# A transformer block with 16 routed experts on one core: the choice of expert 0 in written order, the weight loads around its gather, and four units in plain fp32 where there were six

## The chip, the cores and the metric

One core of a Trainium2 chip. The core has TensorE (PE) for matmuls, VectorE (DVE), ScalarE (ACT), GpSimd (POOL) and a queue engine (SP) that issues transfers; 16 DMA engines move data between HBM and the on-chip memory. The metric is device time of one execution in microseconds (us), the median of several runs.

## The reference

One layer of a hybrid encoder block, for 1024 tokens of 1024 channels, in fp32. A first half (modulated norm, one input projection, a Fourier group and windowed attention, an output projection, a gated residual) gives x2. The second half is the part that matters here:

```
h2  = rmsnorm(x2) * (1 + sc2) + sh2
aff = softmax(h2 @ w_router)                 # 1024 tokens x 16 experts
g, idx = top_k(aff.T, 128)                   # each expert picks its 128 best tokens
xin = h2[idx]                                # gather, 16 x 128 x 1024
y   = (silu(xin @ w_gate) * (xin @ w_up)) @ w_down   # per expert, three 1024 x 1024 matrices
out = x2 + g2 * scatter_add(idx, y * g)
```

The expert weights are 16 x 3 matrices of 4 MB each, read once.

## The kernel before, in words

**Units.** Each 1024 x 1024 expert matrix is cut into four units of 256 rows (1 MB). The units are numbered in the order in which PE uses them: 0 to 3 gate of expert 0, 4 to 7 up of expert 0, 8 to 11 gate of expert 1, 12 to 15 down of expert 0, 16 to 19 up of expert 1, 20 to 23 gate of expert 2, and so on. `load` (L1090) brings the next unit into one of 13 raw buffers. `cut_unit` splits a unit into a high part (ACT, L86) and a low part (DVE, L87) of a reduced fp32 format; a product with split operands is three matmuls for each block (`mm3`, L81 to L83: high by high, high by low, low by high), 12 for a unit. The units in `PLAIN` (0 to 5 before) are not cut: PE multiplies them in plain fp32 (L1263), where the trace shows two matmul records for each block, 8 for a unit.

**Order of work.** `product` is called once for each unit n. It first takes some steps of a generator, `selection` (five steps for each unit with n < 9, three after that), then cuts units up to three ahead, then issues the matmuls. `selection` holds what is still to be done for the other experts while expert 0 runs: 4 empty steps, the split of expert 0's gathered tokens (DVE `t0l`), 3 empty steps, `gather(1)`, then the sort that finds all other experts' thresholds (8 rounds, 1 merge and 6 + 7 + 7 sorting steps, DVE), 7 empty steps, a small matmul (L1227), 7 empty steps, the counting of positions, `gather_a(2)`, 7 empty steps and `gather(2)`; after unit 20 the same for expert 3. That makes 57 steps before the step that issues `gather(2)`. From expert 4 on the gather is issued inside the loop over experts.

**A gather** compares positions with slot numbers (`oneh`, L1277; on DVE for experts 0 to 3, on POOL for the others), multiplies the result with `aux` (token numbers and the gate value in three bf16 parts) on PE (L1285), makes the token numbers (`idx`, DVE L1287), and issues an indirect transfer from POOL (L1289) that reads 128 rows of h2 into `xe` (one buffer). `flip` (L1304) transposes `xe` on PE and splits it; PE reaches the flip of expert e+1 after the third up unit of expert e, which for expert 2 is after unit 18. `put(e)` multiplies by the down matrix (units 12 to 15 for expert 0), scales on ACT (L1318), multiplies by g2 on POOL (L1319, two halves) and issues an indirect scatter-add from POOL (L1322).

**The choice of expert 0.** Attention's last token tile (tile 7) ends in `oproj`. Its two halves of 512 columns are added to x2 on DVE (L791, L792); x2 is transposed (`x2_flip`, L834) and multiplied by the router matrix (L850), then the softmax (L862 to L870) gives the last 128 rows of `aff`. A running sort of the first six tiles (`sorter`) has by then given a list of best values; `choose(0)` (L1168 to L1211) ranks the last two tiles against it and gives the positions of expert 0, then `gather(0)` follows. Tile 7's h2 is finished on DVE between the steps of the choice (`scaled`, L818) and stored by SP (L1242) behind the 11 unit loads that were issued by then (`EARLY` and `LATER`); the load of unit 11 (`HELD`) waits for gather 0's issue by way of a one-element POOL memset. `choose(1)`, expert 1's `oneh` and the cuts of units 6 and 7 follow on DVE.

**What fixes the order.** A scheduler orders each engine's instructions unless `in_order` pins them as written. Before: PE, DVE and POOL from gather 0 to the loop, and all engines inside the loop. The lines quoted are those that set the steps:

```
drain(itertools.islice(rest, 5 if n < 9 else 3))        # product
ahead(min(la, 1 + n // 2))
if u == 2 and e + 1 < NE: xn = flip(gs[e + 1][2], e + 1)  # loop, up units
if 0 < e < NE - 1: drain(put(e - 1, hT))                  # loop, before the up units
```

Of the kernel before, what the change touches and what calls it, by code (L numbers as in the profile page):

```python
# [19 lines left out]
D = 1024  # L20
# [25 lines left out]
def block_kernel(ctx: ExitStack, tc: tile.TileContext, t_in, out):  # L46
# [712 lines left out]
    lastx = []  # L759

    def oproj(t):
# [42 lines left out]
        x2s[t] = x2, rs  # L804

        def normed(c, prev):
            with tc.issue_after(prev.ins):
                DVE.scalar_tensor_tensor(h2[:, c], x2[:, c], rs, G2_r[:, c], op0=OP.mult, op1=OP.mult)
            DVE.tensor_tensor(h2[:, c], h2[:, c], sh2_r[:, c], op=OP.add)

        if t == NT - 1:
            with tc.issue_after(lastadd.ins):
                drain(srt)
            yield from tail(t, 1)

            def scaled(c, prev):
                with tc.issue_after(prev.ins):
                    DVE.scalar_tensor_tensor(h2[:, c], h2[:, c], rs, sh2_r[:, c], op0=OP.mult, op1=OP.add)  # L818

            scaled(slice(0, 512), after["aff"])  # L820
            after["kept"] = lambda kept: scaled(slice(512, D), kept)
        else:
            normed(slice(0, D), cur)
# [13 lines left out]
    def tail(t, b0=0):  # L837
        x2, rs = x2s.pop(t)
        p = None
        for b in range(b0, 2):  # L840
            if b0:
                p = pt()
                for kc in range(4):
                    PE.matmul(p[:, :16], x2Ts[t][:, kc, :], wrG[:, kc, :16], start=(kc == 0), stop=False)
# [3 lines left out]
        if b0:
            for kc in range(4, 8):
                PE.matmul(p[:, :16], x2T[:, kc, :], wrG[:, kc, :16], start=False, stop=(kc == 7))  # L850
        else:

            p = pt()
            for kc in range(8):
                g = 32 * (kc % 4)
                PE.matmul(p[g:g + 32, :128], wrG[:, kc, :], x2T[:, kc, :], start=(kc < 4), stop=(kc >= 4))
            gs_ = p3.tile([128, 128], F32, name="gsum", bufs=1)
            ACT.activation(gs_, p[:, :128], AF.Copy)
            p = pt()
            PE.matmul(p[:, :16], gs_, gsel[:, :16], start=True, stop=True)  # L860
# [6 lines left out]
        ACT.activation(ex, lg, AF.Exp, bias=mx, accum_out=sm)  # L867
# [4 lines left out]
        yield  # L872
# [72 lines left out]
    def sorter():  # L945
# [21 lines left out]
    def filler2():  # L967
        rate[0] = RATE2
        for t in range(NT):
            for i, _ in enumerate(oproj(t)):  # L970
# [4 lines left out]
                for _ in range(2 if t > 4 else 1):  # L975
                    next(srt, None)
# [97 lines left out]
    def load(m=None):  # L1074
# [41 lines left out]
    DVE.tensor_copy(tri, r1_f)  # L1116
# [5 lines left out]
    POOL.memset(ones_b, 1.0)  # L1122
# [42 lines left out]
    def choose(e):  # L1165
# [14 lines left out]
        after.pop("kept", lambda kept: None)(k0)  # L1180
# [53 lines left out]
    gate_parts(0, OLD, DVE)  # L1234
# [45 lines left out]
    def gather(e, oneh=None):  # L1280
        if oneh is None:
            oneh = gather_a(e)
        p = pt()
        for t in range(NT):
            PE.matmul(p[:, :6], oneh[:, t, :], aux[:, t, e, :], start=(t == 0), stop=(t == NT - 1))  # L1285
# [3 lines left out]
        after["p"] = POOL.indirect_dma_start(out=xe, out_offset=None, in_=h2d,  # L1289
                                in_offset=bass.IndirectOffsetOnAxis(ap=idx[:, :1], axis=0))  # L1290
        ax = wk.tile([128, 6], F32, name="ax", bufs=2)
        DVE.tensor_copy(ax, p[:, :6])
        gt = wk.tile([128, 2], F32, name="gt", bufs=4)
        DVE.tensor_tensor(gt[:, 0:1], ax[:, 3:4], ax[:, 4:5], op=OP.add)  # L1294
        after["v"] = DVE.tensor_tensor(gt[:, 1:2], gt[:, 0:1], ax[:, 2:3], op=OP.add)
        gs[e] = idx, gt[:, 1:2], xe
# [29 lines left out]
    tp = traced()  # L1326
    gather(0)
# [30 lines left out]
    in_order(tp, "PE", "DVE", "Pool")  # L1358
    in_order(tsp, "SP")
# [29 lines left out]
    in_order(t2, *PINNED)  # L1389
# [67 lines left out]
```

## Time and profile before

| | us |
|---|---|
| median of 3 runs (983.13 to 985.94) | 984.17 |
| the profiled execution, its own time | 986.08 |
| span of the profiled execution, first to last instruction | 984.3 |
| PE busy, all of the span | 934.3 |
| DVE busy | 788.5 |
| ACT busy | 628.5 |
| POOL busy | 403.9 |

Busy times overlap. A row of the timeline gives start, duration, engine, line, operation, tiles written and read, shapes, count, and in brackets the idle time of the engine before it with what ended it. PEclk is the granted TensorE clock as a share of full speed (2.4 GHz); 0.50 is the lower level (1.2 GHz). Matmuls are pipelined, so a matmul's duration is longer than the distance to the next one. Line numbers are those of the kernel before.

### The profile page before, as it was taken

Reading aid. Unit: us, or ns where it says so; the run is one execution under the profiler, and the core shown is the slowest. Engines: PE = TensorE matmul, PEld = TensorE weight load, DVE = VectorE, ACT = ScalarE, POOL = GpSimd, SP = SyncE. Lnnn points to the kernel's source line nnn. Section 1 sums busy time; section 2 is a strip of 40 time slices with the busy share of each in tenths; the row PEclk is TensorE's granted clock in tenths of the full one; section 3 lists DMA queues with packets and bytes.
Section 4 is the critical chain, followed back from the end, with each engine's and each line's share of the span. In section 5 each row is a group of like instructions: output and inputs, shape, how many; then the busy total and the mean of one; then the engine's idle time right before and its main releaser. Section 6 shows DMA issues by size and latency. Waiting matters only on the chain.

```text
span 984.3 us, 13194 instructions
## 1 busy us (share of the span) xinstructions
PE 934.3 (95%) x4751; PEld 737.0 (75%) x4751; DVE 788.5 (80%) x1238; ACT 628.5 (64%) x838; POOL 403.9 (41%) x240
## 2 busy tenths in 40 slices
PE   4999999989999998799899999999999999999996
PEld 2678776757777776468788888888888888888885
DVE  1436787788777968888888988998898898899894
ACT  2464533667565653147577777777777878777872
POOL 1007465100000001103339768766976976782201
PEclk9999999989999998699899999999999999999998
DMA  8978566462222258699999999999999999999912
GB/s 289 342 254 278 173 214 219 130 190 81 94 77 85 74 193 320 265 406 391 332 341 410 383 386 407 389 386 385 411 386 385 408 386 389 393 403 386 385 72 43
DMA packets 91641, 283.95 MB, mean 288 GB/s; under 512 B 8140, under 2 KB 25728, under 8 KB 91448
## 3 DMA queue, kind: packets, MB, share of 16 engines
q1 hardware_dynamic: 86712, 266.32, 71.1%
q0 software_dynamic: 4864, 16.80, 6.7%
q8 instruction: 37, 0.61, 0.2%
q14 instruction: 28, 0.23, 0.1%
HBM read 263.79 MB, written 21.40 MB: 290 GB/s over the span
## 4 chain that ended last, share of the span: by engine, by line
PE 56%; DMA 1%; DVE 1%; issue 0%; POOLq 0%; ACT 0%; DVEq 0%
PE pa L81 17%; PE pa L83 17%; PE pa L82 17%; PE pt L1304 3%; PE pa L1263 2%; DMA out_dram<-ys,idx 1%; DVE wl L87 0%; DMA xe<-h2d,idx 0%; PE pt L1285 0%; PE pt L1339 0%; POOLq L1453 0%; DVE oneh L1277 0%; DVE ys L1321 0%; PE pa L1149 0%; DVE t1l L87 0%
## 5 line engine op out<-in xcount | busy, mean ns | idle before, releaser
L87 DVE TENSOR_TENSOR wl<-raw,wh 128x2048 fp32r<-128x2048 f32 (+1 forms) x189 | 422.4, 2266 | 55.7 <-ACT wh L86 54.7
L86 ACT ACTIVATE wh<-raw 128x2048 fp32r<-128x2048 f32 (+1 forms) x189 | 355.3, 1896 | 74.8 <-PE pa L82 62.0
L1277 POOL TENSOR_SCALAR oneh<-tri_f,pos 128x128 bf16<-128x128 f32 x96 | 210.4, 2206 | 15.2 <-PE pt L1285 14.7
L81 PE MATMUL pa<-wh,t1h 128*128 128x512 f32 x384 | 151.4, 394 | 0.0
L83 PE MATMUL pa<-wl,t1h 128*128 128x512 f32 x384 | 149.6, 390 | 0.0
L82 PE MATMUL pa<-wh,t1l 128*128 128x512 f32 x384 | 149.5, 389 | 0.0
L81 PE MATMUL pa<-wh,t0h 128*128 128x512 f32 x360 | 143.5, 399 | 0.0
L83 PE MATMUL pa<-wl,t0h 128*128 128x512 f32 x360 | 141.2, 392 | 0.0
L82 PE MATMUL pa<-wh,t0l 128*128 128x512 f32 x360 | 141.2, 392 | 0.0
L83 PEld LDWEIGHTS pa<-wl,t1h 128*128 128x128 f32 x384 | 72.1, 188 | 15.2
L82 PEld LDWEIGHTS pa<-wh,t1l 128*128 128x128 f32 x384 | 72.1, 188 | 14.3
L81 PEld LDWEIGHTS pa<-wh,t1h 128*128 128x128 f32 x384 | 72.1, 188 | 14.3
L803 POOL TENSOR_TENSOR rs<-ss,mhalf 128x1 f32<-128x1 f32 x8 | 4.4, 556 | 185.3 <-DVE ss L801 161.2
L83 PEld LDWEIGHTS pa<-wl,t0h 128*128 128x128 f32 x360 | 68.1, 189 | 14.5
L81 PEld LDWEIGHTS pa<-wh,t0h 128*128 128x128 f32 x360 | 68.3, 190 | 13.7 <-issue 0.2
L82 PEld LDWEIGHTS pa<-wh,t0l 128*128 128x128 f32 x360 | 68.2, 190 | 13.7 <-issue 0.2
L1289 POOL DMA_INDIRECT xe<-h2d,idx x16 | 18.2, 1139 | 139.9 <-DVE gt L1294 133.3
L1319 POOL TENSOR_TENSOR ys<-ys,g_r 128x512 f32<-128x512 f32 x28 | 50.0, 1803 | 46.0 <-ACT ys L1318 46.0
L1322 POOL DMA_INDIRECT out_dram<-ys,idx x15 | 49.3, 3288 | 45.9 <-DVE ys L1321 41.8
L278 ACT ACTIVATE hf<-pt,sh1c,G1c 128x128 f32<-128x128 f32 (+1 forms) x56 | 22.6, 482 | 34.9 <-PE pt L271 34.9
L376 PE MATMUL pu<-wh,hh 128*128 128x512 f32 x128 | 42.6, 417 | 1.0 <-ACT hh L86 0.9
L689 DVE CUSTOM_DVE_ANT_0 sb<-lg,bias,sink 128x384 f32<-128x384 f32 (+1 forms) x64 | 35.3, 579 | 9.9 <-PE lg L687 4.8
(329 smaller groups left out, 1630.8 us busy)
## 6 DMA issues: line engine op xcount, KB each, us to landing
raw<-in_w_gate_dram SPq DMA_DIRECT2D x64, 1024.0 KB, 9.3
raw<-in_w_up_dram SPq DMA_DIRECT2D x64, 1024.0 KB, 8.9
raw<-in_w_down_dram SPq DMA_DIRECT2D x63, 1024.0 KB, 9.1
raw<-in_w_ada_dram SPq DMA_DIRECT2D x16, 1024.0 KB, 7.8
raw<-in_w_ada_dram SPq DMA_DIRECT2D x16, 512.0 KB, 9.6
xt<-in_x_dram SPq DMA_DIRECT2D x8, 512.0 KB
raw<-in_w_out_dram SPq DMA_DIRECT2D x4, 1024.0 KB, 4.9
raw<-in_x_dram SPq DMA_DIRECT2D x8, 512.0 KB
```

Of the source, the lines that this page charges most:

```text
L81: PE.matmul(o, lh, rh, start=start, stop=False)
L82: PE.matmul(o, ll, rh, start=False, stop=False)
L83: return PE.matmul(o, lh, rl, start=False, stop=stop)
L86: ACT.activation(hi, src, AF.Copy)
L87: return (eng or DVE).tensor_tensor(lo, src, hi.bitcast(F32), op=OP.subtract)
L278: ACT.activation(hf[:, a * w:a * w + w], tp[:, a * w:a * w + w], AF.Identity, scale=G1c[:, kc:kc + 1], bias=sh1c[:, kc:kc + 1])
L376: PE.matmul(acc[:, :c1 - c0], lhs, r[kc][:, c0:c1], start=first, stop=(kc == 7 and r is w_l), skip_group_check=c0 == 1024)
L689: DVE.tensor_tensor_reduce(sb[:, :wid], lg[:, :wid], bias[:, kv * 4 + i, j0:j0 + wid], 1.0, sk[:, i:i + 1], op0=OP.add, op1=OP.max, accum_ ...
L1277: (POOL if t < shared else DVE).tensor_scalar(oneh[:, t, :], slots, pos[:, t, e:e + 1], None, op0=OP.is_equal)
L1304: PE.transpose(p[:, k * 128:k * 128 + 128], src[:, (4 * b + k) * 128:(4 * b + k + 1) * 128], ident)
L1319: POOL.tensor_tensor(ys[:, cs_], ys[:, cs_], g2_r[:, cs_], op=OP.mult)
L1322: POOL.indirect_dma_start(out=out2, out_offset=bass.IndirectOffsetOnAxis(ap=idx[:, :1], axis=0), in_=ys, in_offset=None, compute_op=OP.add)
```

## The change

The last tile gets a function of its own (`last_tile`). Its second half goes through the residual, the transposes and ACT's copy in two pieces of 256 columns; its square sum moves from ACT to DVE; the scaling of its h2 moves from DVE to ACT and the addition of sh2 to POOL, with the store in two halves. Small preparations (`tri`, `rank1`, the token part of `aux`) move from DVE to POOL; all gate parts of `aux` move to POOL, behind gather 0, so that gather 0 multiplies by the two token columns alone and expert 0's gate values come from a second small product at the start of `selection`. Expert 1's `oneh` moves into `selection`, behind the split `t0l`. Nine units are loaded before gather 0's end instead of eleven: unit 7 and all behind it wait for the gather's data, by a one-element POOL copy out of `xe`. Units 0 to 3 are plain; 4 and 5 are the two that are cut ahead, 6 and 7 are cut in the loop. `product` takes five steps of `selection` for n < 4 and three after that; the running sort of the last tiles takes four steps at a time for tiles 6 and 7. PE, DVE and POOL are pinned as written from the last tile's first step to the end, SP from the store on, ACT in the loop.

```diff
-EARLY, LATER, HELD = (6, 7, 2, 3, 9, 10), (0, 1, 4, 5, 8), 11
-
-PLAIN = range(6)
-HOME3, HOME2 = (6, 7, 2, 3), (0, 1, 4, 5, 8)
+EARLY, LATER, HELD = (4, 5, 2, 3, 9, 10), (0, 1, 6), 7
+
+PLAIN = range(4)
+HOME3, HOME2 = (4, 5, 2, 3), (0, 1, 6, 7, 8)
...
-    def in_order(start, *engines):
+    def in_order(start, *engines, free=()):
...
-            if e in engines:
+            if e in engines and i.name not in free:
...
+    def last_tile(t, rows, x2, h2, o, ss):
+        mark.append(traced())
+        x2T = x2Ts.pop(t)
+        p = pj()
+        for kc in range(4):
+            PE.matmul(p[:, :16], x2T[:, kc, :], wrG[:, kc, :16], start=(kc == 0), stop=False)
+        for q in range(2):
+            c = slice(512 + 256 * q, 768 + 256 * q)
+            DVE.tensor_tensor(h2[:, c], o[:, 256 * q:256 * q + 256], g1_r[:, c], op=OP.mult)
+            DVE.tensor_tensor(x2[:, c], x2[:, c], h2[:, c], op=OP.add)
+            f = pt()
+            for k in range(2):
+                PE.transpose(f[:, k * 128:k * 128 + 128], x2[:, c.start + k * 128:c.start + k * 128 + 128], ident)
+            ACT.activation(x2T[:, 4 + 2 * q:6 + 2 * q].rearrange("p a b -> p (a b)"), f[:, :256], AF.Copy)
+        for kc in range(4, 8):
+            PE.matmul(p[:, :16], x2T[:, kc, :], wrG[:, kc, :16], start=False, stop=(kc == 7))
+        junk = at0.tile([128, 512], BF, name="junk", tag="qn1")
+        DVE.scalar_tensor_tensor(junk, x2[:, 512:], 1.0 / D, x2[:, 512:], op0=OP.mult, op1=OP.mult, accum_out=ss[:, 1:2])
+        after["ss"] = DVE.tensor_tensor(ss[:, 0:1], ss[:, 0:1], ss[:, 1:2], op=OP.add)
+        rs = p3.tile([128, 1], F32, name="rs", bufs=2)
+        POOL.tensor_tensor(rs, ss[:, 0:1], mhalf[:, 0:1], op=OP.pow)
+        DVE.tensor_tensor(h2[:, 512:], x2[:, 512:], G2_r[:, 512:], op=OP.mult)
+        R, = ranked
+
+        def aside():
+            ACT.activation(h2[:, :512], h2[:, :512], AF.Copy, scale=rs)
+            for b in range(3):
+                DVE.transpose(bestw[32 * b:32 * b + 32, :], R[:, 32 * b:32 * b + 32])
+
+        affinity(t, p, rs, aside)
+        DVE.transpose(bestw[96:, :], R[:, 96:])
+        POOL.tensor_copy(bestT, R[:16])
+        with tc.issue_after(after["exp"].ins):
+            ACT.activation(h2[:, 512:], h2[:, 512:], AF.Copy, scale=rs)
+        for c in (slice(0, 512), slice(512, D)):
+            POOL.tensor_tensor(h2[:, c], h2[:, c], sh2_r[:, c], op=OP.add)
+        lastx.append((rows, x2, h2))
...
-                for _ in range(2 if t > 4 else 1):
+                for _ in range(4 if t > 5 else 2 if t > 4 else 1):
...
-            with tc.issue_after(after["p"].ins):
-                POOL.memset(r[0:1, 0, 0:1], 0.0)
+            POOL.tensor_copy(r[0:1, 0, 0:1], gs[0][2][0:1, 0:1])
...
+    def gate_parts():
+        POOL.memset(aux[:, :, :, 5], 0.0)
+        POOL.tensor_copy(aux[:, :, :, 2], aff)
+        POOL.tensor_tensor(r1, aff, aux[:, :, :, 2], op=OP.subtract)
+        POOL.tensor_copy(aux[:, :, :, 3], r1)
+        POOL.tensor_tensor(r1, r1, aux[:, :, :, 3], op=OP.subtract)
+        POOL.tensor_copy(aux[:, :, :, 4], r1)
...
-    gate_parts(0, OLD, DVE)
     for m in LATER:
         load(m)
     (rows, x2, h2), = lastx
     tsp = traced()
-    gate_parts(OLD, NT, POOL)
-    c0 = choose(0)
-    next(c0)
-    SP.dma_start(h2d[rows, :], h2)
+    for hf in range(2):
+        SP.dma_start(h2d[rows, hf * 512:hf * 512 + 512], h2[:, hf * 512:hf * 512 + 512])
     SP.dma_start(out2[rows, :], x2)
-    drain(c0)
+    drain(choose(0))
...
-        drain(itertools.islice(rest, 5 if n < 9 else 3))
+        drain(itertools.islice(rest, 5 if n < 4 else 3))
...
     gs = {}
-    tp = traced()
-    gather(0)
+    oneh0 = gather_a(0)
+    gather(0, oneh0)
+    gate_parts()
     while len(raws) < NR:
         load()
     SP.dma_start(g2_r, md[3:4, :].to_broadcast([128, D]))
     drain(choose(1))
-    oneh = gather_a(1)
-    cut_unit(2)
-    cut_unit(2)
+    for n, c in (("ax", 4), ("gt", 2)):
+        wk.tile([128, c], F32, name=n, bufs=2 * (4 // c))
+    with tc.issue_after(after["exp"].ins):
+        cut_unit(2)
+        cut_unit(2)
...
     def selection():
+        p = pt()
+        for t in range(NT):
+            PE.matmul(p[:, :4], oneh0[:, t, :], aux[:, t, 0, 2:], start=(t == 0), stop=(t == NT - 1))
+        gates(0, p[:, :4])
         yield from wait(4)
         split(xh, xl, xf)
+        oneh = gather_a(1)
         yield from wait(3)
         gather(1, oneh)
...
     rest = selection()
-    in_order(tp, "PE", "DVE", "Pool")
-    in_order(tsp, "SP")
     t2 = traced()
...
-    in_order(t2, *PINNED)
+    in_order(mark[0], "PE", "DVE", "Pool", free=[i.ins.name for i in aside])
+    in_order(tsp, "SP")
+    in_order(t2, "Activation")
```

`affinity` is the softmax part of `tail`, unchanged, and calls `aside` before the exponential; `gates` is the gate part of `gather`, unchanged but for its columns; `ranked` holds the sort's result.

## Rows read from the trace of the kernel before

**Rows 1.** Windows answer: stretch, length, busy us per engine (instructions), PEclk, DMA share, GB/s.
```profile
478.20:482.10 3.90, 0.34 (x10) 0.31 (x8) 3.90 (x4) 2.50 (x3) 0.00 (x0) 0.77 1.04 418
482.10:487.40 5.30, 5.30 (x15) 4.18 (x14) 2.97 (x6) 0.32 (x1) 5.15 (x6) 0.52 0.96 363
487.40:960.00 472.60, 472.60 (x2274) 391.63 (x2273) 422.55 (x293) 367.61 (x272) 310.54 (x143) 1.00 0.97 371
```

**Rows 2.** Waits, 370 to 500 us: waiter <- releaser: us in total, times, longest.
```profile
PE pt L1285 <- DVE t1l L87: 3.6, 1, 3.6
...
PE pt L1339 <- DMA xe<-h2d,idx: 2.9, 1, 2.9
```

**Rows 3.** Timeline of DVE, 366 to 440 us: start, us, engine, line, operation.
```profile
384.81 0.67 DVE L791 TENSOR_TENSOR raw<-lg,g_r 128x512 f32<-128x512 f32 x1
...
390.52 0.23 DVE L862 SCALAR_TENSOR_TENSOR lg<-pt,rs,cb 128x16 f32<-128x16 f32 x1 [1.20 <-PE pt L850]
...
393.41 0.74 DVE L818 SCALAR_TENSOR_TENSOR raw<-raw,rs,sh_r 128x512 f32<-128x512 f32 x1
...
394.47 0.22 DVE L1187 SCALAR_TENSOR_TENSOR edge<-pa,rank,best 128x1 f32<-128x1 f32 x1
...
398.77 0.22 DVE L1287 TENSOR_SCALAR idx<-pt 128x1 int32<-128x1 f32 x1 [0.28 <-PE pt L1285]
...
405.20 4.62 DVE L87 TENSOR_TENSOR wl<-raw,wh 128x1024 fp32r<-128x1024 f32 x4
...
411.88 0.22 DVE L1287 TENSOR_SCALAR idx<-pt 128x1 int32<-128x1 f32 x1 [0.92 <-PE pt L1285]
```

**Rows 4.** Timeline of PE, 366 to 432 us.
```profile
383.88 0.40 PE L83 MATMUL lg<-wol,yah 128*128 128x512 f32 x1
...
388.53 1.89 PE L850 MATMUL pt<-wrG,x2T 128*128 128x16 f32 x8 [0.69 <-ACT x2T L835]
...
411.81 17.33 PE L1263 MATMUL pa<-raw,ys 128*128 128x512 f32 x40
```

**Rows 5.** Timeline of all engines, 392 to 414 us.
```profile
394.18 0.34 SPq L1242 DMA_DIRECT2D h2d<-raw  x1
...
401.02 1.12 POOL L1289 DMA_INDIRECT xe<-h2d,idx  x1 [6.39 <-DVE junk L1175]
```

**Rows 6.** Groups of DVE, 411.9 to 434.8 us: busy, mean ns | idle before.
```profile
L87 DVE TENSOR_TENSOR wl<-raw,wh 128x2048 fp32r<-128x2048 f32 x2 | 4.6, 2278 | 1.7 <-ACT wh L86 1.7
...
L87 DVE TENSOR_TENSOR t1l<-pt,t1h 128x512 fp32r<-128x512 f32 x2 | 1.3, 686 | 1.0 <-ACT t1h L86 1.0
```

**Rows 7.** Timeline of DVE, 430 to 500 us.
```profile
434.57 0.22 DVE L1224 TENSOR_SCALAR dg<-ident,R 16x16 f32<-16x16 f32 x1
```

**Rows 8.** Timeline of PE, 455 to 492 us.
```profile
459.95 0.39 PE L81 MATMUL pa<-wh,t1h 128*128 128x512 f32 x1
...
468.12 1.04 PE L1304 MATMUL pt<-ident,xe 128*128 128x128 f32 x8
```

**Rows 9.** Timeline of POOL, 450 to 490 us.
```profile
454.10 0.94 POOL L1289 DMA_INDIRECT xe<-h2d,idx  x1 [40.77 <-DVE gt L1294]
460.25 3.61 POOL L1319 TENSOR_TENSOR ys<-ys,g_r 128x512 f32<-128x512 f32 x2 [5.22 <-ACT ys L1318]
464.14 3.38 POOL L1322 DMA_INDIRECT out_dram<-ys,idx  x1 [0.28 <-POOL ys L1319]
482.25 6.82 POOL L1277 TENSOR_SCALAR oneh<-tri_f,pos 128x128 bf16<-128x128 f32 x8 [14.73 <-PE pt L1285]
```

**Rows 10.** Line L1289, 480 to 960 us: gathers of later experts, issue to landing.
```profile
DMA to landing us min/median/max: 7.4/8.0/9.0
```

**Rows 11.** Chain that ended last: start us, us, what.
```profile
401.02 4.34 DMA xe<-h2d,idx
...
967.40 6.64 DMA out_dram<-ys,idx
```

**Rows 12.** The page's part 5: a POOL group beside busy DVE; busy, mean ns.
```profile
L1277 POOL TENSOR_SCALAR oneh<-tri_f,pos 128x128 bf16<-128x128 f32 x96 | 210.4, 2206 | 15.2 <-PE pt L1285 14.7
```

More of the change, by code (lines that the diff above doesn't have):

```diff
@@ L804, in oproj @@
         x2s[t] = x2, rs
[L806 to L823, printed above, removed]
@@ L824, in oproj @@
-        if t < NT - 1:
-            SP.dma_start(h2d[rows, :], h2)
-        else:
-            lastx.append((rows, x2, h2))
+        with tc.issue_after(cur.ins):
+            DVE.scalar_tensor_tensor(h2, x2, rs, G2_r, op0=OP.mult, op1=OP.mult)
+        DVE.tensor_tensor(h2, h2, sh2_r, op=OP.add)
+        SP.dma_start(h2d[rows, :], h2)
+    def last_tile(t, rows, x2, h2, o, ss):
[14 more added lines that the diff above has]
+            PE.matmul(p[:, :16], x2T[:, kc, :], wrG[:, kc, :16], start=False, stop=(kc == 7))
+        junk = at0.tile([128, 512], BF, name="junk", tag="qn1")
+        DVE.scalar_tensor_tensor(junk, x2[:, 512:], 1.0 / D, x2[:, 512:], op0=OP.mult, op1=OP.mult, accum_out=ss[:, 1:2])
[16 more added lines that the diff above has]
+        lastx.append((rows, x2, h2))
@@ L835, in x2_flip, with tail @@
         ACT.activation(x2Ts[t][:, 4 * b:4 * b + 4].rearrange("p a b -> p (a b)"), p, AF.Copy)
-    def tail(t, b0=0):
+    def tail(t):
         x2, rs = x2s.pop(t)
[L839 to L844, printed above, removed]
+        for b in range(2):
             x2_flip(t, b, x2)
@@ L847, in tail, with affinity @@
         x2T = x2Ts.pop(t)
[L848 to L860, printed above, removed]
+        p = pt()
+        for kc in range(8):
+            g = 32 * (kc % 4)
+            PE.matmul(p[g:g + 32, :128], wrG[:, kc, :], x2T[:, kc, :], start=(kc < 4), stop=(kc >= 4))
+        gs_ = p3.tile([128, 128], F32, name="gsum", bufs=1)
+        ACT.activation(gs_, p[:, :128], AF.Copy)
+        p = pt()
+        PE.matmul(p[:, :16], gs_, gsel[:, :16], start=True, stop=True)
+        affinity(t, p, rs)
+        yield
+    def affinity(t, p, rs, aside=None):
         lg = p3.tile([128, 16], F32, name="lg", bufs=2)
@@ L952, in sorter @@
         R = yield from halve(R)
-        for b in range(4):
-            DVE.transpose(bestw[32 * b:32 * b + 32, :], R[:, 32 * b:32 * b + 32])
-        DVE.tensor_copy(bestT, R[:16])
+        ranked.append(R)
     def wo_cut():
@@ L1115, in block_kernel @@
     SP.dma_start(r1_f, t_in["k_tri"][0])
-    DVE.tensor_copy(tri, r1_f)
+    aside = [POOL.tensor_copy(tri, r1_f)]
     tri_f = rt.tile([128, 3, 128], F32, name="tri_f")
@@ L1121, in block_kernel @@
     ones_b = rt.tile([128, 128], BF, name="ones_b")
[L1122 removed]
+    aside.append(POOL.memset(ones_b, 1.0))
     tok = rt.tile([128, NT, 2], F32, name="tok")
@@ L1278, in gather_a, with gather @@
         return oneh
-    def gather(e, oneh=None):
-        if oneh is None:
-            oneh = gather_a(e)
+    def gather(e, oneh):
+        n = 6 if e else 2
         p = pt()
         for t in range(NT):
-            PE.matmul(p[:, :6], oneh[:, t, :], aux[:, t, e, :], start=(t == 0), stop=(t == NT - 1))
+            PE.matmul(p[:, :n], oneh[:, t, :], aux[:, t, e, :n], start=(t == 0), stop=(t == NT - 1))
         idx = wk.tile([128, 1], I32, name="idx", bufs=4)
@@ L1288, in gather, with gates @@
         xe = wk.tile([128, D], F32, name="xe", bufs=1)
[L1289 removed]
+        POOL.indirect_dma_start(out=xe, out_offset=None, in_=h2d,
                                 in_offset=bass.IndirectOffsetOnAxis(ap=idx[:, :1], axis=0))
[L1291 to L1292 removed]
+        gs[e] = idx, None, xe
+        if e:
+            gates(e, p[:, 2:6])
+    def gates(e, p):
+        ax = wk.tile([128, 4], F32, name="ax", bufs=2)
+        DVE.tensor_copy(ax, p)
         gt = wk.tile([128, 2], F32, name="gt", bufs=4)
[L1294 to L1296 removed]
+        DVE.tensor_tensor(gt[:, 0:1], ax[:, 1:2], ax[:, 2:3], op=OP.add)
+        DVE.tensor_tensor(gt[:, 1:2], gt[:, 0:1], ax[:, 0:1], op=OP.add)
+        gs[e] = gs[e][0], gt[:, 1:2], gs[e][2]
     def flip(src, e):
```

36 lines of the change are left out of this document (17 added, 19 removed).

## The prediction

> **What bounds the kernel now.** I read the windows answer first. From 487.4 to 960 us PE is busy in all of its 472.6 us at full clock: a thread of matmuls that nothing else interrupts [rows 1]. So what is won or lost before expert 3 moves the end by as much, and only places where PE stands still, or runs at half clock, are to be looked at. The waits have two such places. PE waits for expert 0's gathered rows (end of the choice, 2.9 us of wait behind a long stretch of small work), and for 3.6 us at the product of gather 3, on a DVE flip half [rows 2]. The windows show that second one as 0.34 us busy in 3.9, and after it 5.3 us at a granted clock of 0.52, that is, mostly the 1.2 GHz level [rows 1]: another 2.6 us, so that gather 3 costs 6.2 in all.
>
> The timeline of the choice shows a chain through all engines: last matmul of tile 7 (383.88 + 0.40), DVE's additions to x2 (from 384.81), the router product at half clock (388.53, 1.89 us), the softmax (390.52), the last ranking steps (edge at 394.47), idx at 398.77, gather issued at 401.02, rows there 4.34 us later [rows 3, 4, 5, 11]. idx is finished at 398.99; the gather left 2.0 us after it, having waited for h2's store, which SP issued at 394.18 behind the last of eleven unit loads [rows 3, 5].
>
> **The change part by part.** All times are on the axis of the profiled execution (986.08 us; span 984.3 and 1.8 around it). It lies 1.9 above the median of 984.17; I add differences to the median.
>
> *Tile 7's tail and the choice.* DVE starts 0.5 us after PE's last matmul because sorting steps stand there, and its two operations on the last half have the sort's transposes between them. In pieces: start at about 384.4, four operations of 256 columns at half of 0.67 plus a dependent start, some 0.4 each, end 386.0. Two transposes instead of four, half a copy: the router product, of the same eight matmuls in 0.9 to 1.9 us, ends near 388.1, softmax at 388.2 in place of 390.5: 2.3 earlier. The 0.74 us that L818 takes in the choice goes to ACT; the edge gains 0.3 more, since the added best-list transposes run while ACT does the exponential. idx moves by -2.6 us. Bounds: -0.5 (four sorting steps at a time crowd DVE in tiles 6 and 7) and -3.3 [rows 3, 4].
>
> *Store and gather 0.* Two unit loads fewer stand ahead of the store, at 2.6 us each (1 MB at the 400 GB/s or so of the busy windows [rows 1]), so it ends by the new idx (396.4). Gather 0 leaves at about 396.7 and its rows are there at 401.0, 4.3 earlier. This is not what reaches PE's weights, next.
>
> *DVE up to gather 1.* From idx 0 to idx 1 DVE takes 13.1 us (398.77 to 411.88) [rows 3]: choice of expert 1, its `oneh`, 4.62 of cuts, the split. The same list stands in the new order; only `oneh` comes after the split, so PE's product for gather 1, written behind unit 0, now waits for all of it. Idx 1 is at 409.3, again -2.6; unit 0 ends at about 408. So 1.7 of the 4.3 is lost as a wait on PE. The moved gate parts (six POOL operations behind gather 0) and the extra eight small matmuls lie in the 5 us until the rows land, at 0.85 us an operation as in the `oneh` group that ran mostly beside an idle DVE (6.82 for 8 [rows 9]).
>
> *Loads.* Units 7, 8, 11, 12 leave near 403.5 and have 15 us or more before they are cut. Nothing; 2.6 us each if that cover were gone.
>
> *Two units cut instead of plain.* Plain: 17.33 for 40 records, 8 for a unit, 3.47 [rows 4]. Cut: three units from 459.95 to 468.12, 2.72 each [rows 8]. PE saves 2 x 0.75 = 1.5. DVE and ACT get two cuts more, at 2.28 on DVE [rows 6], and the cuts of 6 and 7 come where the sort is. DVE's list from idx 1 to `dg` (the operation behind the sort) was 22.9 us (411.88 to 434.79 [rows 3, 7]); without two cuts (4.6), their ACT wait (1.7), a flip half and its wait (1.3 and 1.0), 14.3 is the sort and its like [rows 6]. With the slower pace `dg` stands in unit 9, behind the cuts of 6 to 11: 14.3 + 6 x 2.28 + 1.3 (flip) + 1.3 (expert 0's product) = 30.6 us, and the cut of 12 and the flip half that frees PE's transposing buffer bring 33.5. PE is at unit 11 after 3 x 3.47 + 7 x 2.72 + 2 flips of 0.9 = 31.2. So DVE is late by about 2.3, where before it had room. I take 2.4; bounds 0 and 5. Units 11 to 15 and two small products of the counting are 5 x 2.72 + 1.2 = 14.8; unit 15 ends at idx 1 + 31.2 + 2.4 + 14.8 = 48.4 (before: 459.95 - 411.88 = 48.1 [rows 3, 8]), so at 457.8, 2.2 earlier than before: the 1.5 saved is eaten by the backlog.
>
> *The pace of `selection`.* This is the large term. 57 steps stand ahead of gather 2. Before, n = 0 to 8 take 45, n = 9 to 12 twelve: gather 2 falls into unit 13, and POOL issues it at 454.10 [rows 9], before `put(0)` is written. After, n = 0 to 3 take 20, n = 4 to 15 36: 56, so gather 2 falls into unit 16. On POOL's pinned queue it now stands behind `put(0)`: two multiplies (460.25, 3.61 us) and the scatter (464.14, 3.38 us) [rows 9], which begin only when unit 15 ends (459.95). POOL is free 7.6 us after unit 15, the gather leaves at 7.75, and lands 8.0 later (median of the thirteen later gathers, 7.4 to 9.0 [rows 10]): unit 15 + 15.75. PE comes to expert 2's flip after units 16 to 18, 8.5 after unit 15. It stands for 7.2 us. The flip starts at 457.8 + 15.75 = 473.5, before 468.12 [rows 8]: **+5.4**. Bounds of the landing: 4.34 as for gather 0 on an idle machine [rows 11], and 11.1 if the scatter's transfers, 6.64 from issue on a quiet end [rows 11], go first.
>
> *What the stop costs behind it.* After 3.6 us of standing, PE had 5.3 us at half clock [rows 1]; after 7.2 I take the same on 4.4 us: +2.2 (1.6 to 2.7).
>
> *Gather 3's stall.* PE comes to it later against DVE's list (flip half, cut, product, `oneh`, two cuts, flip half), which is unchanged: -1.5; bounds 0 and -6.2.
>
> Sum: +5.4 + 2.2 - 1.5 = **+6.1 us**: 990.3.
>
> A rule that speaks against the moved work: POOL's `oneh` operations take 2.21 us on average [rows 12], against 0.85 in the stretch of mostly idle DVE [rows 9]. The Trainium skill, "SBUF — State Buffer", section "SBUF: two separate sides", says that DVE operations with two SBUF inputs and GpSimd ones share a port pair under an exclusive lock, and the later one waits for the whole instruction. These rows agree in direction. The cuts are such operations, and by the rule the six gate parts would each wait for one (rival C).
>
> **The rivals.**
> - **A, one stall replaces the other: faster.** DVE works its backlog off in gaps and the drained queues let gather 2 land in 4.34. Unit 15 then ends at 409.3 + 31.2 + 14.8 = 455.3, the flip starts 12.1 later, at 467.4 (-0.7); +2.2 of clock; gather 3's stall and its half clock, 6.2, are gone: -4.7, 979.5. For it: front gains of 2.6 and 1.5 are real, and a long stop on PE lets DVE catch up. Against: later gathers never landed under 7.4 [rows 10]. It decides if PE starts expert 2's flip before 470.6.
> - **B, stall as forecast, gather 3 free: no change.** +5.4 + 2.2 - 6.2 = +1.4, 985.6. Against: DVE's list between the two is the same length.
> - **C, POOL blocked.** Six gate parts at 2.21 from 397.8 end at 411; the gate product on PE stands ahead of unit 0, which then ends 6 later than DVE allows; 2.4 of it pays DVE's backlog: +9.7, 993.9.
> - **D, the gather queues behind the scatter.** Its packets start when the scatter's are through (464.14 + 6.64 = 470.8, not 467.7): +3.1, in all +9.2, 993.4. The Trainium skill, "DMA: Bandwidth & Descriptors", section "Queues, rings and completion order", says that descriptors of one ring are taken in order, which is D; no row here has a gather directly behind a scatter.
> - That the change does not do what it says: the counts of steps follow from the code, and before's (gather 2 in unit 13) agrees with POOL's 454.10, one and a half units ahead of unit 16's 459.95 with idx behind the cuts [rows 8, 9]; I leave it nothing.
>
> **How the numbers follow.** Forecast 0.45, A 0.22, B 0.13, C 0.08, D 0.12. A change within 0.3% (2.95 us) can't be told from none. Slower: forecast, C and D, 0.65; same: B, 0.13; faster: A, 0.22. The forecast's own range is 987 to 994 (backlog 0 to 5, landing 4.34 to 11.1, one at its end at a time). The range for 8 in 10 cuts A's lower half and the sum of two bad ends: 979.5 to 996.5.
>
> **What would show it.** Right: PE idle for 5 us or more directly ahead of expert 2's flip (L1304's `xe`), released by a gather that POOL issues behind the scatter; a half-clock stretch after it; idx 0 some 2.6 earlier against tile 7's last matmul; PE waiting for DVE at gather 1 and around unit 11. Wrong: expert 2's flip without a wait, or gather 2 ahead of the scatter on POOL; then A or better holds.

## The result and the profile after

The changed kernel takes 997.25 us (median of six runs, 995.02 to 997.93) against 984.95 for the kernel before (six runs, 983.13 to 986.54): ratio 1.0115, 95% interval 1.0103 to 1.0127, that is 12.3 us slower. The forecast was +6.1. The profiled execution took 995.02, its span is 993.2. One execution of before_g3, a kernel further down, took 2383.70 us for a reason that nothing here shows; it counts in the median given there (988.29 without it) and not in the ratio.

The waits of PE between 360 and 500 us (waiter <- releaser: us in total, times, longest), for [rows 2]:

```profile
PE pt L1323 <- DMA xe<-h2d,idx: 10.1, 1, 10.1
PE pt L1245 <- DVE t0l L87: 2.9, 1, 2.9
...
PE pt L1299 <- DVE t1l L87: 1.7, 1, 1.7
PE pt L1299 <- DVE oneh L1292: 1.4, 1, 1.4
PE pt L1361 <- DMA xe<-h2d,idx: 1.3, 1, 1.3
```

L1323 is the flip (before L1304), L1299 the product of a gather (L1285), L1245 the small product behind the sort (L1227), L1361 expert 0's transposes (L1339). The 1.4 for `oneh` is at gather 0 (392.07 in PE's timeline below), where the kernel before waited 1.07; no wait of that list is at gather 1. The wait at gather 3 shrank from 3.6 to 1.7 and the one for expert 0's rows from 2.9 to 1.3; a new one of 2.9 stands behind the sort and a new one of 10.1 at expert 2's flip.

POOL's timeline, 383 to 500 us, for [rows 5, 9]:

```profile
385.71 2.50 POOL L852 TENSOR_TENSOR raw<-raw,sh_r 128x512 f32<-128x512 f32 x2 [0.59 <-ACT raw L842]
394.18 1.14 POOL L1303 DMA_INDIRECT xe<-h2d,idx  x1 [5.97 <-DVE idx L1301]
...
395.54 0.75 POOL L1153 CAST aux<-aff 128x128 bf16<-128x128 f32 x1
396.38 0.49 POOL L1154 TENSOR_TENSOR r<-aff,aux 128x128 f32<-128x128 f32 x1
...
458.35 3.81 POOL L1338 TENSOR_TENSOR ys<-ys,g_r 128x512 f32<-128x512 f32 x2 [49.36 <-ACT ys L1337]
462.44 3.45 POOL L1341 DMA_INDIRECT out_dram<-ys,idx  x1 [0.28 <-POOL ys L1338]
466.20 1.25 POOL L1303 DMA_INDIRECT xe<-h2d,idx  x1 [0.30 <-issue]
```

Gather 2 (466.20) stands behind `put(0)`'s multiplies and scatter; before it left ahead of them. The chain that ended last (start us, us, what) gives its landing, 10.56 us later, and what it released:

```profile
466.20 10.56 DMA xe<-h2d,idx
476.80 1.97 PE pt L1323 x8
```

PE's timeline: tile 7's last matmul, the product of gather 0, expert 0's transposes, the product of gather 1, the product behind the sort, and the first record behind unit 15, for [rows 4, 8]:

```profile
380.17 0.40 PE L83 MATMUL lg<-wol,yah 128*128 128x512 f32 x1
...
392.07 1.56 PE L1299 MATMUL pt<-aux,oneh 128*128 128x2 bf16 x8 [1.44 <-DVE oneh L1292]
...
398.69 1.61 PE L1361 MATMUL pt<-ident,xe 128*128 128x128 f32 x5 [1.27 <-DMA xe<-h2d,idx]
...
405.95 0.99 PE L1299 MATMUL pt<-aux,oneh 128*128 128x6 bf16 x8
...
441.33 0.51 PE L1245 MATMUL pt<-dg,ones 16*128 16x16 f32 x2 [2.94 <-DVE t0l L87]
...
458.06 0.35 PE L1299 MATMUL pt<-aux,oneh 128*128 128x6 bf16 x8
```

DVE's timeline, for [rows 3, 7]: start of the last tile's additions, the softmax's first and last operation, expert 0's edge, idx 0, the first cuts, idx 1, and the end of the sort:

```profile
381.23 0.41 DVE L825 TENSOR_TENSOR raw<-lg,g_r 128x256 f32<-128x256 f32 x1
...
385.09 0.23 DVE L883 SCALAR_TENSOR_TENSOR lg<-pj,rs,cb 128x16 f32<-128x16 f32 x1 [0.64 <-PE pj L832]
...
386.29 0.72 DVE L893 TENSOR_SCALAR aff<-ex,rsm 128x16 f32<-128x16 f32 x1
...
388.99 0.22 DVE L1205 SCALAR_TENSOR_TENSOR edge<-pa,rank,best 128x1 f32<-128x1 f32 x1
...
393.66 0.22 DVE L1301 TENSOR_SCALAR idx<-pt 128x1 int32<-128x1 f32 x1 [0.28 <-PE pt L1299]
...
406.99 0.22 DVE L1301 TENSOR_SCALAR idx<-pt 128x1 int32<-128x1 f32 x1 [0.28 <-PE pt L1299]
...
438.26 0.22 DVE L1242 TENSOR_SCALAR dg<-ident,R 16x16 f32<-16x16 f32 x1
438.41 2.27 DVE L87 TENSOR_TENSOR wl<-raw,wh 128x2048 fp32r<-128x2048 f32 x1
440.61 1.27 DVE L87 TENSOR_TENSOR t0l<-pt,t0h 128x512 fp32r<-128x512 f32 x2
```

Windows of the main stall, what follows it, the two shorter stretches at the lower clock, and the rest, for [rows 1] (same columns):

```profile
466.70:476.80 10.10, 0.00 (x0) 0.00 (x0) 2.08 (x1) 0.00 (x0) 0.75 (x1) 0.60 1.03 338
476.80:482.40 5.60, 5.60 (x17) 4.74 (x18) 2.54 (x3) 3.00 (x3) 0.00 (x0) 0.50 0.24 97
...
487.40:960.00 472.60, 470.87 (x2265) 389.93 (x2265) 421.82 (x295) 364.70 (x271) 315.52 (x148) 1.00 0.99 376
...
441.40:444.90 3.50, 3.50 (x9) 2.82 (x10) 3.50 (x5) 0.00 (x0) 0.00 (x0) 0.51 1.03 411
...
492.60:496.10 3.50, 3.50 (x10) 2.72 (x9) 2.15 (x1) 0.40 (x1) 3.50 (x3) 0.51 0.93 328
```

PE does nothing for 10.1 us, then works 5.6 us at half clock. From 487.4 on it is busy throughout, as before, but for the wait of 1.7 us at gather 3 and 3.5 us at half clock behind it; so what is lost ahead of the flip stays lost.

**Where the axes differ.** The two profiled spans differ by 8.9 us, the medians by 12.3. Tile 7's last matmul ends at 380.57, before at 384.28 [rows 4], 3.7 us earlier, though little of the change stands ahead of it. Some 3.4 of it are the clock of that one execution (19.00 us at 0.82, an estimate from the rows below): before's PEclk falls in a stretch of the attention where after's does not. The windows, of before and then of after:

```profile
199.00:218.00 19.00, 15.08 (x64) 10.11 (x65) 14.84 (x51) 11.14 (x31) 0.31 (x1) 0.82 0.73 221
```

```profile
199.00:215.00 16.00, 12.54 (x68) 8.22 (x69) 14.13 (x48) 10.63 (x31) 0.00 (x0) 1.00 0.73 229
```

The profiled execution of after is the fastest of its six runs, that of before near its slowest. From tile 7's end on, after loses 8.9 + 3.7 = 12.6 us, which agrees with the medians; below I count from there, in "marks": tile 7's end, idx 0, idx 1, end of unit 15 (458.06; before 459.95), flip of expert 2 (476.80; before 468.12), end.

### The profile page after: what moved, and what is told of

The parts are those of the page before. It is cut to its first block, busy times and chain, and to the rows that moved or that the text cites. A ratio compares the mean times of both kernels' runs of the same rounds, so it can differ in the third digit from the quotient of the medians.

```text
span 993.2 us, 13252 instructions
## 1 busy us (share of the span) xinstructions
PE 934.2 (94%) x4767; PEld 738.1 (74%) x4767; DVE 793.7 (80%) x1233; ACT 633.3 (64%) x841; POOL 408.7 (41%) x246
## 4 chain that ended last, share of the span: by engine, by line
PE 49%; DMA 2%; DVE 1%; issue 0%; POOLq 0%; DVEq 0%
PE pa L81 16%; PE pa L83 15%; PE pa L82 15%; PE pt L1323 3%; DMA xe<-h2d,idx 1%; DMA out_dram<-ys,idx 1%; DVE wl L87 0%; PE pt L1299 0%; POOLq L1480 0%; DVE ys L1340 0%; DVE oneh L1292 0%; DVE t1l L87 0%; DVEq L87 0%; DVEq L1340 0%; POOLq L1341 0%
## 5 line engine op out<-in xcount | busy, mean ns | idle before, releaser
L87 DVE TENSOR_TENSOR wl<-raw,wh 128x2048 fp32r<-128x2048 f32 (+1 forms) x191 | 427.1, 2266 | 54.4 <-ACT wh L86 53.4
L86 ACT ACTIVATE wh<-raw 128x2048 fp32r<-128x2048 f32 (+1 forms) x191 | 359.1, 1895 | 79.6 <-PE pa L82 63.9
L81 PE MATMUL pa<-wh,t0h 128*128 128x512 f32 x368 | 146.3, 397 | 0.0
L83 PE MATMUL pa<-wl,t0h 128*128 128x512 f32 x368 | 144.1, 392 | 0.0
L82 PE MATMUL pa<-wh,t0l 128*128 128x512 f32 x368 | 143.9, 391 | 0.0
```

The source lines that it names most:

```text
L81: PE.matmul(o, lh, rh, start=start, stop=False)
L82: PE.matmul(o, ll, rh, start=False, stop=False)
L83: return PE.matmul(o, lh, rl, start=False, stop=stop)
L86: ACT.activation(hi, src, AF.Copy)
L87: return (eng or DVE).tensor_tensor(lo, src, hi.bitcast(F32), op=OP.subtract)
```

## Experiments

Theory P: the loss is gather 2's place on POOL behind `put(0)`, and the pace of `selection` puts it there. Theory B: the loss is DVE's backlog, from the two added cuts. Every comparison is with the kernel before, run on the same chip.

**pace5: the change with one more unit at five steps.**

```diff
-        drain(itertools.islice(rest, 5 if n < 4 else 3))
+        drain(itertools.islice(rest, 5 if n < 5 else 3))
```

> The changed kernel with five steps of selection for n < 5 in place of n < 4: one unit's pace, two steps. Gather 2 falls into unit 15, so on POOL it stands ahead of put(0)'s multiplies and scatter. Theory P (the loss is gather 2's place behind put(0)): the 10.1 us wait at expert 2's flip goes but for 0 to 2 us, gather 2 leaves POOL before unit 16 starts, and the time falls from 997.3 to 986 to 989. Theory B (the loss is DVE's backlog from the two added cuts, and the flip only waits because everything is late): one unit earlier gives at most a third of the way, 993 or more.

Measured: 985.49 against 985.48, ratio 0.9999 (0.9989 to 1.0010). POOL's timeline:

```profile
457.13 0.94 POOL L1303 DMA_INDIRECT xe<-h2d,idx  x1 [46.18 <-DMA raw<-in_w_up_dram]
458.25 3.69 POOL L1338 TENSOR_TENSOR ys<-ys,g_r 128x512 f32<-128x512 f32 x2 [0.18 <-ACT ys L1337]
462.22 3.38 POOL L1341 DMA_INDIRECT out_dram<-ys,idx  x1 [0.28 <-POOL ys L1338]
```

Two more steps of a generator, which bring the gather out one unit earlier, 0.2 us before POOL takes up `put(0)`, are worth all of the 12 us. That is a net figure: the wait behind the sort is also shorter (1.8 us for 2.9, with no fall of the clock behind it), and gather 3's is back at 3.6. P's wait is gone as said; how much of the 12 is the backlog's, this run alone does not tell.

**pace9: the change with the pace of before (`n < 9`).**

> The changed kernel with five steps for n < 9, as in the kernel before. Gather 2 falls into unit 13. Theory P: no wait at expert 2's flip; the sort stands in more of the cuts, so PE waits up to 4 us for DVE around unit 8; 984 to 988. Theory B: with the two added cuts the faster pace makes DVE's backlog larger, and the time stays above 990.

Measured: 987.05, ratio 1.0018 (1.0007 to 1.0029). Gather 2 leaves earlier still (453.67), but PE now waits 3.1 us for `dg` at L1245 and has 3.4 us at half clock behind it: more steps early crowd DVE. It is the backlog that B speaks of, and the time is some 1.5 us over pace5's.

**before_pace4: the kernel before with the change's pace alone.**

```diff
-        drain(itertools.islice(rest, 5 if n < 9 else 3))
+        drain(itertools.islice(rest, 5 if n < 4 else 3))
```

> The kernel before with nothing changed but the pace: five steps for n < 4 in place of n < 9. Theory P: gather 2 falls into unit 16 behind put(0), expert 2's flip waits 8 to 11 us, 994 to 998, so the pace alone is the whole loss. Theory B: six plain units leave DVE room, the time stays within 3 us of 985.

Measured: 998.05, ratio 1.0135 (1.0115 to 1.0155). The first waits of PE, then POOL's timeline:

```profile
PE pt L1304 <- DMA xe<-h2d,idx: 9.7, 1, 9.7
```

```profile
460.95 3.80 POOL L1319 TENSOR_TENSOR ys<-ys,g_r 128x512 f32<-128x512 f32 x2 [47.94 <-DMA raw<-in_w_up_dram]
465.03 3.44 POOL L1322 DMA_INDIRECT out_dram<-ys,idx  x1 [0.28 <-POOL ys L1319]
468.77 1.26 POOL L1289 DMA_INDIRECT xe<-h2d,idx  x1 [0.30 <-issue]
```

The stall comes without any other part of the change: the pace alone gives it, and a loss of the same size.

**defer_scatter: the change, with `put(0)`'s scatter issued behind gather 2.** The two multiplies stay ahead of the gather.

> The changed kernel with put(0)'s scatter issued behind gather 2 in place of ahead of it; the two multiplies stay ahead. Gather 2 leaves POOL some 3.7 us earlier (the scatter's 3.45). Theory P with rival D (the gather's transfers also queue behind the scatter's): landing falls from 10.5 to about 8 us, the flip wait from 10.1 to about 4, the time by 6 to 991. P without D (the transfers are slow for another reason): landing stays at 10.5, the time falls by 3.7 to 993.5. Theory B: no change.

Measured: 989.63, ratio 1.0049 (1.0032 to 1.0067). The gather leaves at 464.66; its landing in the chain:

```profile
464.66 8.18 DMA xe<-h2d,idx
```

PE waits 3.8 us in place of 10.1. Pace, cuts and choice are those of the change, and 7.6 of the 12.3 us are gone. Of the 6.3 us that PE waits less, 3.9 come from the earlier issue (3.9 us behind POOL's first multiply in place of 7.85) and 2.4 from the landing (8.18 in place of 10.56).

The records of single DMA packets in the traces show what the scatter in front does. In the change, the scatter's packets of 4 KB (0.33 us each) start from 468.97 to 473.21, and the first of the gather's (0.16 us each) starts at 472.27, 6.1 us behind the gather's issue, when most of the scatter's are through. Gather 2 of the kernel before and of pace5, with no scatter in front, has its first packet 4.2 us behind the issue and lands 8.5 and 7.4 us behind it. So some 1.9 us of the landing are a wait behind the scatter's packets. In defer_scatter the first packet comes no sooner (6.3 us, of which POOL spends 2.93 on the issue), but all are through in 1.5 us in place of 3.9; why, no run here shows. The Trainium skill, "DMA: Bandwidth & Descriptors", section "Queues, rings and completion order", says for the queues of SP and ACT that each DMA engine takes descriptors in ring order; the packets here, from POOL's queue, agree.

**choice_alone: the change's last tile and choice, with the plain units, homes, loads and pace of before.**

```diff
-EARLY, LATER, HELD = (4, 5, 2, 3, 9, 10), (0, 1, 6), 7
-PLAIN = range(4)
-HOME3, HOME2 = (4, 5, 2, 3), (0, 1, 6, 7, 8)
+EARLY, LATER, HELD = (6, 7, 2, 3, 9, 10), (0, 1, 4), 5
+PLAIN = range(6)
+HOME3, HOME2 = (6, 7, 2, 3), (0, 1, 4, 5, 8)
...
-        drain(itertools.islice(rest, 5 if n < 4 else 3))
+        drain(itertools.islice(rest, 5 if n < 9 else 3))
```

> The changed kernel with six plain units and the pace of the kernel before (five steps for n < 9); nine units are still loaded ahead of gather 0, unit 5 is the first behind it. So the choice in written order alone. Theory P: the choice is worth the 1.2 us that the trace of the changed kernel shows between tile 7's last matmul and idx 1, and DVE has room for the sort: 983.5 to 984.5 (ratio 0.998 to 0.9995). Rival: the 3.0 us by which the rows of gather 0 are earlier reach PE in full: 982.5 (0.997).

Measured: 983.67 against 984.98, ratio 0.9983 (0.9975 to 0.9992): 1.3 us faster (0.8 to 2.5 by the interval), half of what the prediction gave the choice.

**cuts_alone: the kernel before with the change's plain units, homes and load lists, pace of before.**

```diff
-EARLY, LATER, HELD = (6, 7, 2, 3, 9, 10), (0, 1, 4, 5, 8), 11
-PLAIN = range(6)
-HOME3, HOME2 = (6, 7, 2, 3), (0, 1, 4, 5, 8)
+EARLY, LATER, HELD = (4, 5, 2, 3, 9, 10), (0, 1, 6, 7, 8), 11
+PLAIN = range(4)
+HOME3, HOME2 = (4, 5, 2, 3), (0, 1, 6, 7, 8)
```

> The kernel before with four plain units in place of six, pace and choice as before (units 4 and 5 are cut ahead, 6 and 7 in the loop). PE saves 1.5 us. Theory P with the DVE backlog: the sort then stands among the cuts and PE waits 3 to 4 us for DVE around units 8 to 11, so 1 to 3 us slower: 986.5 to 988. Rival: DVE has room, 1.5 us faster: 984.

Measured: 989.51, ratio 1.0049 (1.0036 to 1.0062), worse than expected. The longest wait of PE, and the windows behind it:

```profile
PE pt L1227 <- DVE dg L1224: 4.0, 1, 4.0
```

```profile
436.40:443.20 6.80, 4.73 (x12) 3.85 (x13) 6.76 (x12) 0.00 (x0) 0.00 (x0) 0.50 1.02 407
```

DVE is the bound while the sort runs; two more cuts there make PE wait 4.0 us. The clock falls 2.0 us before the wait ends (438.47), and 4.8 us of work behind it run at half clock. B is real by itself, 4.5 us at before's pace, but it does not give the 12.

**Gather 3's stall.** In pace5, PE still waits 3.6 us at gather 3, for a transposing buffer that DVE holds. Two steps more ahead of it should end that:

```diff
-            yield from wait(7)
+            yield from wait(7 if e == 2 else 9)
```

> The changed kernel with five steps for n < 5, and gather 3 issued two steps later, in unit 23 in place of 22, so that a whole unit of products stands between expert 1's second flip and the product of gather 3. Theory: that product waits for a transposing buffer that DVE's flip half frees 3.6 us later; with a unit between, the wait and the half clock behind it (some 2.6 us) go: 979.5 to 981.5. Rival: DVE is what PE waits for there, and the wait moves to the next unit's cut: 985.

Measured: 987.78, ratio 1.0028 (1.0016 to 1.0039), above theory and rival: the theory falls. The same edit on the kernel before:

> The kernel before with gather 3 issued two steps later, in unit 23. Same theory and rival as for the one before: 979.5 to 981 if the wait and the half clock go, 985 if the wait moves. Against the other this shows whether four plain units and the new choice are worth anything once both stalls are gone.

Measured: 988.46, ratio 1.0034 (1.0023 to 1.0044). Of before_g3, PE's longest wait and POOL's timeline:

```profile
PE pt L1304 <- DMA xe<-h2d,idx: 5.3, 1, 5.3
```

```profile
480.02 17.08 POOL L1277 TENSOR_SCALAR oneh<-tri_f,pos 128x128 bf16<-128x128 f32 x8 [14.72 <-PE pt L1285]
497.26 3.13 POOL L1289 DMA_INDIRECT xe<-h2d,idx  x1 [0.16 <-issue]
```

Of the stall at L1285 0.8 us of 3.6 are left, and with the rest went DVE's idle time. POOL's `oneh` of expert 4 stands ahead of gather 3 in POOL's order; it takes 17.08 us, with DVE busy in 14.13 of them, where it took 6.82 [rows 9], with DVE busy in 2.86. So the gather leaves late and expert 3's flip waits. It is the main stall once more, at another gather. Single operations of that group, the first beside a cut of DVE, the second with no cut running:

```profile
482.80 2.71 POOL L1277 TENSOR_SCALAR oneh<-tri_f,pos 128x128 bf16<-128x128 f32 x1
482.82 2.29 DVE L87 TENSOR_TENSOR wl<-raw,wh 128x2048 fp32r<-128x2048 f32 x1
...
495.93 0.60 POOL L1277 TENSOR_SCALAR oneh<-tri_f,pos 128x128 bf16<-128x128 f32 x1
```

The one beside the cut ends 0.4 us behind the cut's end. The Trainium skill, "SBUF — State Buffer", section "SBUF: two separate sides", puts DVE and GpSimd on a shared port pair under an exclusive lock; the 2.71 against 0.60 and the 17.08 against 6.82 agree.

**The two edits together: gather 3 two steps later, and expert 4's `oneh` written behind it.** In four kernels:

```diff
-            yield from wait(7)
+            yield from wait(7 if e == 2 else 9)
...
-            if u == 0 and 1 < e < NE - 2:
+            if u == (3 if e == 2 else 0) and 1 < e < NE - 2:
                 oneh = gather_a(e + 2)
```

> The kernel before, with gather 3 issued two steps later (unit 23 in place of 22, so that its matmuls do not ask for a PSUM tile that DVE's split of the flip of hs still holds) and with POOL's eight oneh of expert 4 written behind gather 3 in place of ahead of it. In the run with the later gather alone (988.46 us) the 3.6 us wait at L1285 went, but gather 3 left POOL at 497.26 behind 17.1 us of oneh and the flip of expert 3 waited 5.3 us with 6.8 us at half clock. Theory P (what costs is a gather standing behind other work in POOL's pinned queue): gather 3 now leaves within 2 us of idx, at about 484, lands by 493 ahead of the flip at 502; the wait of 3.6 and its half clock (6.8 us at half speed: 3.4 more) go, nothing takes their place: 985 - 3.6 - 2.6 = 978 to 980. Rival (the wait moves on to the next resource whatever the order, as in the run before this): POOL's oneh beside a busy DVE stand ahead of put(1)'s products and scatter, expert 4's gather or the flip is late, 984 or more.

Measured: 980.72 against 985.87, ratio 0.9958 (0.9943 to 0.9973). POOL's timeline and the window answering to the first two of [rows 1]:

```profile
482.11 0.99 POOL L1289 DMA_INDIRECT xe<-h2d,idx  x1 [17.41 <-DVE gt L1294]
483.14 13.99 POOL L1277 TENSOR_SCALAR oneh<-tri_f,pos 128x128 bf16<-128x128 f32 x8
```

```profile
478.00:482.10 4.10, 3.27 (x22) 2.73 (x22) 4.07 (x7) 2.02 (x2) 0.00 (x0) 1.00 1.02 405
482.10:487.40 5.30, 5.30 (x25) 4.38 (x24) 5.27 (x5) 3.71 (x3) 5.25 (x3) 1.00 1.02 403
```

The long `oneh` is still 13.99 us, but nothing that PE waits for stands behind it; the clock stays at 1.00. 5.2 us are won, and 980.72 is a little over the expected 978 to 980: PE waits 0.8 us here and 1.5 at expert 4's gather, which had no wait before.

> The change's choice of expert 0 with the weights' plan of before (983.67 us by itself), with gather 3 two steps later and expert 4's oneh behind it on POOL. Theory P, with effects that add: 983.7 - 3.6 (the PE wait at gather 3, its L1299) - 1.3 to 2.6 (the 3.4 us of half clock behind it and what goes with it) = 977.5 to 979. Rival (the wait moves on): 983 or more, with another PE wait of 3 us or more between 480 and 520 us.

Measured: 981.55, ratio 0.9964 (0.9951 to 0.9977), 2.5 us over what was expected and 1.5 under the rival's: the effects don't add in full.

> The whole change with the pace of 5 for five units (985.49 us by itself: gather 2 ahead of put(0) on POOL), with gather 3 two steps later and expert 4's oneh behind it on POOL. Theory P: 985.5 - 3.6 - 1.3 to 2.6 = 979 to 981, so the change's choice and its four plain units with both queues in order are 4 to 6 us faster than before. Against the run of the choice alone with the same two edits it should stay 1.5 to 2 us behind (the two added cuts of DVE: the wait at L1245 for t0l of 1.8 us). Rival (the wait moves on): 985 or more.

Measured: 981.20, ratio 0.9960 (0.9947 to 0.9974), 0.2 over what was expected; the 1.5 to 2 us behind choice_g3o are not there.

> As the choice alone with gather 3 later and oneh behind it, and gather 1's matmuls three steps (three fifths of a unit) later, so that PE does not wait the 1.4 us for DVE's oneh there. If PE's wait is what counts: 1.0 to 1.5 us less than the same without it, 976 to 978. Rival (DVE is what counts in that stretch: the sort's steps behind gather 1 start later and gather 2 with them): the same time or up to 2 us more, since gather 2 leaves POOL at 453 with 5 us to spare ahead of put(0).

, with this edit besides:

```diff
-        yield from wait(3)
+        yield from wait(6)
         gather(1, oneh)
```

Measured: 980.63, ratio 0.9956 (0.9942 to 0.9971). The expectation took the 1.4 us of the waits for a wait at gather 1; the timeline has it at gather 0, which this edit does not touch, and it is still 1.4. At gather 1 there was next to nothing to win: the eight matmuls of its product took 0.42 us in choice_g3o and take 0.34 here. The 0.9 us between the medians can't be told from none (980.69 to 982.52 against 979.90 to 981.95), so the run does not decide between the two.

All four are faster than the kernel before by 4 to 5 us, and their intervals overlap: whether the change's choice adds its 1.3 us to the repaired gather 3 can't be told from these runs. Expert 4's gather, now the next wait, wasn't tried.

## Why the forecast was right in kind and wrong in size

| from mark to mark | forecast | measured |
|---|---|---|
| tile 7's end to idx 1 | -2.6 | -1.2 |
| idx 1 to end of unit 15 | +0.3 | +3.0 |
| unit 15 to expert 2's flip | +7.6 | +10.6 |
| flip to end | +0.7 | +0.2 |
| sum | +6.0 | +12.6 |

The mechanism was right: gather 2 in unit 16, behind `put(0)` on POOL, PE idle ahead of L1323, half clock after it. What failed are three sizes of the sum: the gain of the choice (1.4 us too much), the cost of the two cuts (2.7 too little, the half clock behind their wait left out) and the landing behind the scatter (2.6 of the 3.0 by which the stall was too small). Together with the last row they are the 6.6 us between forecast and measurement. The choice's gain, the wait for DVE and the landing each came within their own bounds, but the range held only one bad end at a time.

- ***Tile 7's tail and the choice*** was oversized: idx 0 came 1.4 earlier against tile 7's end (13.09 in place of 14.49 us), not 2.6. DVE still began 0.66 us after PE, behind sorting steps. The softmax's first operation came 1.7 earlier, not 2.3. From the edge to idx 0 another 0.4 went (4.67 us, before 4.30). The softmax's last operation took 0.72 us beside POOL's moved additions (L852; that they are the cause is not shown); before it took 0.23:

```profile
391.63 0.23 DVE L870 TENSOR_SCALAR aff<-ex,rsm 128x16 f32<-128x16 f32 x1
```

  Gather 0's rows came 3.0 earlier against that mark (PE's transposes start at 398.69, before at 405.40), idx 1 only 1.2. Of the 1.8 between, 0.2 are the second small product, 0.9 a slower unit 0 (granted clock 0.71 over it, before 0.85) and 0.7 the forecast wait for `oneh` at gather 1, whose eight matmuls took 0.99 us (405.95), before 0.34. The forecast had put 1.7 down to that wait alone.
- ***DVE up to gather 1*** passed the lost gain on: idx 1 is 1.2 earlier; choice_alone's 1.3 agrees.
- ***Two units cut instead of plain*** failed by what it left out. The wait for DVE was forecast at 2.4 us and came at 2.94, at the place named. But behind it stand 3.5 us at a clock of 0.51, 1.7 us that the step didn't price, though it priced half clock behind the other stall: 2.9 + 1.7 - 1.5 saved = 3.1 of the 3.0 measured. Another 0.5 is a slip of the sum: it set the new stretch, added up from rates, against the old one as measured (48.1); by the same rates the old one is 47.6, so the step's own terms, 2.4 - 1.5, made +0.9 and not +0.3. cuts_alone shows wait and half clock again, with a wait of 4.0.
- ***The pace of `selection`***: right in place, and the gather left POOL 8.14 us behind unit 15 for the forecast 7.75. The landing was mis-sized: 10.56 us against the 8.0 of gathers with no scatter directly in front. That is rival D (chance 0.12), 2.6 of its 3.1: the packets show the gather's behind the scatter's, for some 1.9 us.
- ***What the stop costs behind it***: 5.6 us at half clock from the flip on, for 4.4 forecast and the 5.3 of [rows 1], though the wait was almost three times as long as that one's 3.6. Gather 3's wait shrank as said, by more: 1.9 less wait and some 0.8 less half clock (3.5 us for 5.3) against the 1.5 forecast. The 0.6 that the first had too little and the 1.2 that the second had too little partly cancel, so that this row came nearest is in part luck.
- Rival A is out: the gather took 10.56 us, not 4.34. B came in part: gather 3's wait is 1.7, not gone. C is false: the gate parts took 0.49 to 0.75 us each on POOL (395.54 and on), in the cover that the prediction named.

## What to carry to other kernels

Where an engine's order is pinned, a generator's pace decides which instruction stands in front of which; count the steps to each transfer and compare them with the next work of that engine, since two steps too late cost 12 us here, and two steps later at the next gather 2 to 3.5. A wait that was taken away here handed its time to the next in line: gather 3 gave nothing until the POOL work ahead of it was moved too. Look for half clock behind every wait of PE that a forecast adds, not only behind the largest: here it was 1.7 us behind a wait of 2.9. Three sizes fell on their bad side at once, and a range that allowed one at a time was too narrow.

## Hardware behaviour not expected

- A gather of 128 rows took 7.4 and 8.5 us to land with no scatter-add in front (gather 2 of pace5 and of the kernel before), 8.18 with one behind it, and 10.56 (before_pace4: 10.1) with one in front.
- Issuing a gather occupied POOL for 0.9 to 1.3 us, but for 2.9 to 3.1 where a cut of DVE had just begun (before_g3: 3.13 us from 497.26, cut from 497.18 to 499.47). Issuing a scatter-add took 3.4 us beside such cuts and 1.6 with none running (before_g3, at 506.35).
- The same POOL operation took 0.60 us by itself and 2.7 beside a cut of DVE; eight of them took 6.8 to 18.5 us (18.51 in the kernel before, at 516.30, with DVE busy for 17.33).
- A wait of PE of 2.9 us was followed by 3.5 us at a clock of 0.51, one of 4.0 by 4.8 us at 0.50, one of 10.1 by 5.6 us at 0.50. One of 1.7 (gather 3 of the change) was followed by 3.5 us at 0.51, one of 1.8 (pace5, behind the sort) by no fall.
- Two executions of the same attention code differed in clock (0.82 and 1.00 in the stretch shown), so that a mark behind it moved by microseconds that the change had no part in.
